# All of gate's block products in matmuls of 512 columns, in one run, with another order of the products

## The chip, the cores and the metric

The kernel runs on one core of a Trainium2 chip. The metric is the device time of one execution in microseconds (us), the median of the runs. The core has a matrix engine (TensorE, PE in the profile; its weight loads are listed apart as PEld), VectorE (DVE), ScalarE (ACT), GpSimd (POOL) and the queues that issue DMA transfers (SP's and POOL's here). Matrix results go to PSUM, of which the kernel uses eight banks of 128 partitions x 512 fp32 columns; everything else stands in SBUF.

## The reference

A decoder trunk of two layers on one sequence of 512 positions and 1024 channels, all in fp32. Each layer has a normalised mixer with a residual and then a normalised gated feed-forward part with a residual. The change touches the feed-forward part alone:

```python
def gated_conv_ffn(x, w_gate, w_up, conv_w, conv_b, w_down):
    g = jnp.einsum('bsd,df->bsf', x, w_gate)
    g = causal_dwconv3(g, conv_w) + conv_b
    up = jnp.einsum('bsd,df->bsf', x, w_up)
    return jnp.einsum('bsf,fd->bsd', jax.nn.silu(g) * up, w_down)
...
        hn = rms_norm(h, norm_ffn[layer])
        h = h + gated_conv_ffn(hn, w_ffn_gate[layer], w_ffn_up[layer], conv_ffn[layer],
                               b_conv_ffn[layer], w_ffn_down[layer])
```

`w_gate` and `w_up` are 1024 x 2816, `w_down` is 2816 x 1024, and `causal_dwconv3` is a convolution over three positions in each channel.

## The kernel before

*Precision.* An fp32 value is held as a high and a low part. A product of two such values is three matmuls that add up in one PSUM bank: high x high, high x low and low x high (`mm3`, lines 154 to 157). A part is made in one of two ways. `halves` (line 721) copies the high part on ACT and subtracts on DVE. `summed` (line 136) writes the negated value on ACT with rounding, adds the value to it by a POOL transfer with addition (line 142), and copies the high part on ACT.

*Tiling.* The 2816 channels are 22 rows of 128. Rows 0 and 1 are computed directly (`direct`). The others are done in pairs, f = 2, 4, ... 20: the 1024 input channels and the 512 positions are cut in two as well, and each of gate (`g`) and up (`u`) becomes a 2x2 block product that takes seven products of blocks instead of eight (Strassen's method in Winograd's form). One product is 256 positions wide and runs over four pairs of channel tiles (`kp` from 0 to 3). After each pair, `half_down` multiplies half of the output channels by four rows done earlier: 48 matmuls of 512 columns, L155 to L157 (two rows and 24 matmuls at f = 2 and 4). Each layer so has ten stages of fourteen block products and a half down projection; the last down products stand behind them (`d_last` in layer 0, a block product at L1262 in layer 1).

*A product* (`multiply`, line 562 on). In the narrow form it is twelve matmuls of 256 columns into the first half of a bank (L577). In the form with `both`, the moving operand holds high and low part side by side, so that one matmul of 512 columns does high x high into the first half of the bank and high x low into the second (L568), and a matmul of 256 columns does low x high (L570); the two alternate over `kp`, four of each. Its second half must be added to the first afterwards. From f = `FIRST_WIDE` = 6 on, products 2, 5 and 3 of both keys take that form.

*Banks.* Each key has three banks for a pair: `BANK` gives "a" to products 1, 6, 7 and 4, "e" to 5 and 3, and "b" to 2. Products of one bank follow each other in it, some of them adding to the sum that stands there; between them the bank is read out. Seven banks circulate (`ps_mm`, line 43) among all matmuls.

*Reading out* (`products`, line 766 on). ACT copies products 1, 6, 7 and 4 of gate into two padded rows and 1, 6 and 7 of up into `kept` (L789). DVE adds product 2 onto 1, the bank of 5 onto 7 and 3 onto 6 (L783), in two additions of 128x256 where the product has two halves. Up's product 4 is read out of its bank by the multiplication with the gate (L813). After products 4 and 3 of gate a row is scaled, convolved (ACT L610, DVE L612) and goes through silu (ACT L620). `split_acts` makes high and low parts of four finished rows at a time (ACT L264, DVE L266).

*Operands.* `block_sums` (line 671 on) makes the moving sums once per layer: `t41` for products 4 and 5, with high and low part side by side, and `t23` for 6 and 7, as one tile of high parts and one of low parts. For `kp` 0 and 1 the low part is made as in `summed` (ACT L692, POOL L693, ACT L694), for 2 and 3 by `halves`. The parts of the plain activations stand in `hg2`, both side by side. `prepare` (line 725) makes the stationary sides of one pair during the stage before it: `a11` (product 1), `s12` (5 and 6), the raw second half (2 and 4, by `summed`) and `s34` (7 and 3), each high and low part of 128x1024, in buffers that circulate by sixes.

*Order.* Every engine and queue runs its instructions in an order fixed when the program is built. A scheduler derives it from the program's order, the data and the buffers; `behind` adds an order between two instructions without a wait on data.

Of the kernel before, what the change touches and what calls it, by code (L numbers as in the profile page):

```python
# [9 lines left out]
F32R = mybir.dt.float32r  # L10
BF16 = mybir.dt.bfloat16
AF = mybir.ActivationFunctionType
ALU = mybir.AluOpType
PSUM = bass.MemoryType.PSUM

P = 128
# [15 lines left out]
def tile_trunk(ctx: ExitStack, tc: tile.TileContext, x, norm_mix, norm_ffn, final_norm,  # L32
# [521 lines left out]
    def multiply(banks, name, product, left, right, both=None):  # L554

        at = BANK[product]  # L560
        first = at not in banks
        if first:
            banks[at] = mm_bank(f"{name}{at}")
        ps = banks[at][:, :HALF]
        if both is not None:
            for kp in range(NP):
                (a_hi, a_lo), last = left(kp), kp == NP - 1
                nc.tensor.matmul(banks[at], a_hi, both(kp), start=first and kp == 0, stop=last,  # L568
                                 skip_group_check=True)
                nc.tensor.matmul(ps, a_lo, right(kp)[0], start=False, stop=last,  # L570
                                 skip_group_check=True)
            return banks[at]
        for kp in range(NP):
            (a_hi, a_lo), (b_hi, b_lo) = left(kp), right(kp)
            for l, r, end in ((a_hi, b_hi, False), (a_hi, b_lo, False),
                              (a_lo, b_hi, kp == NP - 1)):
                nc.tensor.matmul(ps, l, r, start=first, stop=end, skip_group_check=True)  # L577
                first = False
        return ps
# [8 lines left out]
    class Ffn:  # L588
# [81 lines left out]
        def block_sums(self, kp):  # L670
# [14 lines left out]
            self.t23[kp] = self.sums(kp)  # L685
            t41 = self.ap.tile([P, 2, 2, HALF], F32R, name=f"t41_{n}")
            self.t41[kp], self.t41both[kp] = (t41[:, 0], t41[:, 1]), t41
            for (hi, lo), src in ((self.t41[kp], t[:, 2:, :]), (self.t23[kp], t[:, :2, :])):
                if kp > 1:
                    self.halves(hi, lo, src)  # L690
                    continue
                behind(nc.scalar.activation(lo, src, AF.Copy, scale=-1.0), self.first_sums)  # L692
                nc.gpsimd.dma_start(lo, src, accum_op=ALU.add)  # L693
                behind(nc.scalar.activation(hi, src, AF.Copy), self.first_sums)  # L694

        def moving(self, product, kp):
# [3 lines left out]
                c = slice(HALF, S) if product == 3 else slice(0, HALF)  # L700
                return hg[k][0][:, c], hg[k][1][:, c]
            if product in (6, 7):
                return tuple(t[:, product - 6, :] for t in self.t23[kp])
            return tuple(t[:, {4: 0, 5: 1}[product], :] for t in self.t41[kp])

        def moving_both(self, product, kp):
            if product == 5:
                return self.t41both[kp][:, :, 1, :]
            return hg2[kp + NP][:, :, HALF:] if product == 3 else hg2[kp + NP][:, :, :HALF]

        def multiply(self, banks, name, product, weights_, both):
            hi, lo = weights_
# [12 lines left out]
        def prepare(self, f):  # L725
# [12 lines left out]
            for key in "gu":  # L738
# [19 lines left out]
                    c = slice(i * P, (i + 1) * P)  # L758
                    stat[key, product] = hi[:, :, c], lo[:, :, c]
                w = self.unit(f"s34{key}_{n}")  # L760
                self.halves(*w, s34)
                put(key, 7, w, 0)
                put(key, 3, w, 1)
            return stat
# [1 line left out]
        def products(self, f, stat):  # L766
# [6 lines left out]
            dst = {("g", 1): pads[0][:, lo], ("g", 6): pads[0][:, hi], ("g", 7): pads[1][:, hi],  # L773
                   ("g", 4): pads[1][:, lo]}
            dst.update({("u", product): kept[:, i, :] for i, product in enumerate((1, 6, 7))})
            onto = {2: 1, 5: 7, 3: 6}
            s, pending = {}, {}

            wide = f >= FIRST_WIDE

            def add(dst_, ps):
                for half in range(1 + wide):
                    ins = nc.vector.tensor_tensor(dst_, ps[:, half * HALF : (half + 1) * HALF],  # L783
                                                  dst_, ALU.add)
                return ins

            def after(key, product, ps):
                if (key, product) in dst:
                    nc.scalar.copy(dst[key, product], ps)  # L789
                elif product == 5 and (key, 7) not in pending:  # L790
                    pending[key, 5] = ps
                elif product in onto:
                    add(dst[key, onto[product]], ps)
                if (key, product) == ("u", 4):
                    pending["u", 4] = ps
                if product == 7:
                    self.added[key] = add(dst[key, 7], pending[key, 5])

            for key, product in (("g", 1), ("u", 1), ("g", 5), ("g", 6), ("u", 5), ("u", 6),
                                 ("g", 2), ("g", 7), ("u", 2), ("u", 7), ("g", 4), ("g", 3),  # L800
                                 ("u", 4), ("u", 3)):
                after(key, product, self.multiply(banks[key], f"{key}{n}", product,
                                                  stat[key, product],
                                                  wide and product in onto))
                if (key, product) in (("g", 4), ("g", 3)):
                    j = product == 4
                    row = pads[j][:, 2:]
# [2 lines left out]
                    if j and layer == 0:  # L810
                        nc.vector.tensor_tensor(s[1], s[1], self.r, ALU.mult)
            nc.vector.tensor_tensor(s[1][:, HALF:], kept[:, 2, :], s[1][:, HALF:], ALU.mult)
            nc.vector.tensor_tensor(s[1][:, :HALF], pending["u", 4], s[1][:, :HALF], ALU.mult)  # L813
            if layer == 0:
                nc.vector.tensor_tensor(kept[:, :2, :], kept[:, :2, :],
                                        self.r.rearrange("p (a b) -> p a b", a=2), ALU.mult)
# [38 lines left out]
    def ffn0(norm):  # L855
        nonlocal prm1
        with tc.tile_pool(name="f0", bufs=1) as ap:
            def sums(kp):
                return [ap.tile([P, 2, HALF], F32R, name=f"t23{i}_{kp}") for i in "hl"]

            ffn = Ffn(0, prm0, norm, ap, sums)
            def half_down(a, b, half):
# [540 lines left out]
```

## Time and profile before

| | |
|---|---|
| runs | 981.34, 981.38 and 981.81 us, median 981.38 |
| the profiled execution | 981.97 us, its span 980.2 us |
| mean granted TensorE clock | 0.998 |
| instructions | 14798 |
| moved by DMA | 129.27 MB |

The span runs from the first to the last instruction of that one execution, and its own time holds 1.8 us around the span. Busy times of engines overlap, so they don't add up to the span. Matmuls are pipelined, and a matmul's own duration (390 ns for 512 columns) is longer than the time from its start to the next one's; what PE needs for a chain of matmuls is read from start to start.

### The profile page before, as it was taken

To read this page: it belongs to the slowest core of one execution; us is meant where nothing else is said; L and a number is where in the kernel's file an instruction comes from. 1 tells how busy PE (TensorE), PEld (TensorE's weight loads), DVE (VectorE), ACT (ScalarE), POOL (GpSimd) and SP (SyncE) were. 2 spreads that over 40 slices of the span, in tenths; PEclk is the share of its full clock that TensorE was granted. 3 is DMA by queue.
4 is the path that set the end of the run, shared out by engine and by line. 5 is a ranking of instruction groups with operands and counts; after the bars stand their busy time and mean duration, and the time that the engine had idled before them with its cause. 6 is when DMAs were issued, how large, how long until landed. Compare 5 with 4: busy or idle time off the path is not lost.

```text
span 980.2 us, 14798 instructions
## 1 busy us (share of the span) xinstructions
PE 971.0 (99%) x5712; PEld 859.6 (88%) x5712; DVE 808.8 (83%) x1279; ACT 559.2 (57%) x839; POOL 113.0 (12%) x131
## 2 busy tenths in 40 slices
PE   9999999999999999999999999999999999999996
PEld 7888888999988899888889988889989988999885
DVE  5887458998899888997986765599988889878897
ACT  5523347765555564655488734586655455554675
POOL 2141023000000000000210001210000000000022
PEclk9999999999999999999999999999999999999999
DMA  7442225555455455553414623265555554545574
GB/s 249 146 136 86 87 87 129 139 146 147 129 151 135 124 144 136 137 145 107 129 49 117 213 74 103 55 145 132 148 157 137 138 134 124 153 131 147 151 152 128
DMA packets 88371, 129.27 MB, mean 132 GB/s; under 512 B 4485, under 2 KB 58477, under 8 KB 88301
## 3 DMA queue, kind: packets, MB, share of 16 engines
q1 hardware_dynamic: 78316, 98.69, 32.4%
q0 software_dynamic: 8208, 27.79, 15.1%
q10 hardware_dynamic: 1776, 1.84, 0.7%
q8 instruction: 45, 0.74, 0.3%
q14 instruction: 26, 0.20, 0.1%
HBM read 98.42 MB, written 2.10 MB: 103 GB/s over the span
## 4 chain that ended last, share of the span: by engine, by line
PE 92%; DVE 4%; ACT 2%; issue 1%; DMA 0%; POOLq 0%; DVEq 0%; ACTq 0%; POOL 0%
PE d L155 3%; PE dn L155 3%; PE d L156 3%; PE d L157 3%; PE dn L156 3%; PE dn L157 3%; PE gu L155 2%; PE gu L157 1%; PE oo L157 1%; PE oo L155 1%; PE gu L156 1%; PE oe L157 1%; PE oe L155 1%; PE oo L156 1%; PE oe L156 1%; PE u_4a L577 1%
## 5 line engine op out<-in xcount | busy, mean ns | idle before, releaser
L612 DVE SCALAR_TENSOR_TENSOR c<-rows,prm,c 128x512 f32<-128x512 f32 x88 | 65.4, 746 | 2.4 <-ACT c L610 2.3
L142 POOL DMA_DIRECT2D wlo_g<-raw_g x20 | 17.2, 860 | 382.4 <-ACT wlo_g L140 303.0
L155 PE MATMUL d<-a_hi,whi_d 128*128 128x512 f32 x144 | 56.2, 390 | 0.0
L155 PE MATMUL dn<-whi_dn,a_hi 128*128 128x512 f32 x144 | 56.1, 390 | 0.0
L157 PE MATMUL d<-a_hi,wlo_d 128*128 128x512 f32 x144 | 56.1, 389 | 0.0
L156 PE MATMUL d<-a_lo,whi_d 128*128 128x512 f32 x144 | 56.1, 389 | 0.0
L156 PE MATMUL dn<-wlo_dn,a_hi 128*128 128x512 f32 x144 | 56.0, 389 | 0.0
L157 PE MATMUL dn<-whi_dn,a_lo 128*128 128x512 f32 x144 | 56.0, 389 | 0.0
L264 ACT ACTIVATE a_hi<-s 128x512 fp32r<-128x512 f32 x40 | 25.1, 628 | 28.9 <-PE d L157 10.0
L722 ACT ACTIVATE whi_s12u<-s12u 128x1024 fp32r<-128x1024 f32 x20 | 21.2, 1058 | 32.7 <-DVE s12u L744 32.7
L620 ACT ACTIVATE s<-c,prm 128x512 f32<-128x512 f32 x44 | 31.5, 719 | 11.3 <-DVE c L612 11.1
L200 ACT ACTIVATE hg<-h,prm 128x512 fp32r<-128x512 f32 x24 | 17.3, 723 | 36.1 <-DVE h L313 36.1
L723 DVE TENSOR_TENSOR wlo_s34u<-s34u,whi_s34u 128x1024 fp32r<-128x1024 f32 x20 | 24.5, 1225 | 16.1 <-ACT whi_s34u L722 16.1
L151 DVE TENSOR_TENSOR wlo_dn<-raw_dn,whi_dn 128x1024 fp32r<-128x1024 f32 x18 | 22.0, 1225 | 18.7 <-ACT whi_dn L150 18.6
L142 POOL DMA_DIRECT2D wlo_u<-raw_u x21 | 18.1, 860 | 162.2 <-ACT wlo_u L140 132.9
L211 POOL TENSOR_TENSOR ssq_f<-ssq_f,sq_f 128x512 f32<-128x512 f32 x14 | 19.7, 1409 | 133.9 <-ACT sq_f L210 98.9
L201 DVE SCALAR_TENSOR_TENSOR hg<-h,prm,hg 128x512 fp32r<-128x512 f32 x24 | 25.0, 1045 | 11.1 <-ACT hg L200 11.1
L610 ACT ACTIVATE c<-rows,prm 128x512 f32<-128x512 f32 x44 | 31.2, 711 | 2.2 <-DVE rows L808 2.2
L157 PEld LDWEIGHTS d<-a_hi,wlo_d 128*128 128x128 f32 x144 | 27.0, 188 | 5.8
L155 PEld LDWEIGHTS d<-a_hi,whi_d 128*128 128x128 f32 x144 | 27.0, 188 | 5.7
L157 PEld LDWEIGHTS dn<-whi_dn,a_lo 128*128 128x128 f32 x144 | 27.0, 188 | 5.7
L155 PEld LDWEIGHTS dn<-whi_dn,a_hi 128*128 128x128 f32 x144 | 27.0, 188 | 5.7
(1327 smaller groups left out, 3594.0 us busy)
## 6 DMA issues: line engine op xcount, KB each, us to landing
raw_g<-in_w_ffn_gate_dram SPq DMA_DIRECT2D x40, 512.0 KB, 3.8
raw_u<-in_w_ffn_up_dram SPq DMA_DIRECT2D x40, 512.0 KB, 4.1
raw_dn<-in_w_ffn_down_dram SPq DMA_DIRECT2D x22, 512.0 KB, 3.6
wlo_u<-raw_u POOLq DMA_DIRECT2D x21, 512.0 KB, 5.2
wlo_g<-raw_g POOLq DMA_DIRECT2D x20, 512.0 KB, 4.6
raw_d<-in_w_ffn_down_dram SPq DMA_DIRECT2D x18, 512.0 KB, 3.5
raw_oe<-in_w_out_even_dram SPq DMA_DIRECT2D x8, 512.0 KB, 3.5
raw_v<-in_w_in_odd_dram SPq DMA_DIRECT2D x8, 512.0 KB, 4.2
```

Of the source, the lines that this page charges most:

```text
L142: nc.gpsimd.dma_start(lo, raw, accum_op=ALU.add)
L151: behind(nc.vector.tensor_tensor(lo, raw, hi.bitcast(F32), ALU.subtract), after[0])
L155: nc.tensor.matmul(ps, lhs[0], rhs[0], start=start, stop=False)
L156: nc.tensor.matmul(ps, lhs[0], rhs[1], start=False, stop=False)
L157: nc.tensor.matmul(ps, lhs[1], rhs[0], start=False, stop=stop)
L201: nc.vector.scalar_tensor_tensor(hg[k][1], h[k], g, hg[k][0].bitcast(F32), op0=ALU.mult, op1=ALU.subtract)
L264: nc.scalar.activation(hi, src, AF.Copy, scale=scale)
L610: nc.scalar.activation(c, t[:, 0:S], AF.Copy, scale=prm("cf", ft))
L612: nc.vector.scalar_tensor_tensor(c, t[:, i : S + i], prm("cf", i * NF + ft), c, op0=ALU.mult, op1=ALU.add)
L620: nc.scalar.activation(s, c, AF.Silu, bias=self.prm("bf", ft))
L722: nc.scalar.activation(hi, src, AF.Copy)
L723: nc.vector.tensor_tensor(lo, src, hi.bitcast(F32), ALU.subtract)
```

## The change

- `multiply` with `both` issues its four matmuls of 512 columns one after another, and then its four of 256.
- From f = 6 on, all seven products of gate take that form; of up still 2, 5 and 3.
- `t23` becomes one tile for each of products 6 and 7, with high and low part side by side. The splits of those sums are two pieces of 128x256 instead of one of 128x512.
- The fourteen products come in another order.

| | order |
|---|---|
| before | g1 u1 g5 g6 u5 u6 g2 g7 u2 u7 g4 g3 u4 u3 |
| after | g1 u1 g5 g2 g6 u5 u6 u2 g7 u7 g3 u3 g4 u4 |

- Product 5 is copied by ACT and 7 is added onto it by DVE; before it was the other way round. Where a copied product has a second half, DVE adds that half to the copy.
- From f = 6 on, the low part of gate's `s34` is made by a negation on ACT and a POOL transfer with addition, no longer by DVE.
- Up's product 4 is the last one and is still read out of its bank.

```diff
@@ -564,10 +564,10 @@
         ps = banks[at][:, :HALF]
         if both is not None:
             for kp in range(NP):
-                (a_hi, a_lo), last = left(kp), kp == NP - 1
-                nc.tensor.matmul(banks[at], a_hi, both(kp), start=first and kp == 0, stop=last,
-                                 skip_group_check=True)
-                nc.tensor.matmul(ps, a_lo, right(kp)[0], start=False, stop=last,
+                nc.tensor.matmul(banks[at], left(kp)[0], both(kp), start=first and kp == 0,
+                                 stop=kp == NP - 1, skip_group_check=True)
+            for kp in range(NP):
+                nc.tensor.matmul(ps, left(kp)[1], right(kp)[0], start=False, stop=kp == NP - 1,
                                  skip_group_check=True)
             return banks[at]
         for kp in range(NP):
@@ -685,7 +685,8 @@
             self.t23[kp] = self.sums(kp)
             t41 = self.ap.tile([P, 2, 2, HALF], F32R, name=f"t41_{n}")
             self.t41[kp], self.t41both[kp] = (t41[:, 0], t41[:, 1]), t41
-            for (hi, lo), src in ((self.t41[kp], t[:, 2:, :]), (self.t23[kp], t[:, :2, :])):
+            for (hi, lo), src in ((self.t41[kp], t[:, 2:, :]), *(
+                    ((both[:, 0], both[:, 1]), t[:, i, :]) for i, both in enumerate(self.t23[kp]))):
                 if kp > 1:
                     self.halves(hi, lo, src)
                     continue
@@ -700,13 +701,16 @@
                 c = slice(HALF, S) if product == 3 else slice(0, HALF)
                 return hg[k][0][:, c], hg[k][1][:, c]
             if product in (6, 7):
-                return tuple(t[:, product - 6, :] for t in self.t23[kp])
+                t = self.t23[kp][product - 6]
+                return t[:, 0, :], t[:, 1, :]
             return tuple(t[:, {4: 0, 5: 1}[product], :] for t in self.t41[kp])
 
         def moving_both(self, product, kp):
-            if product == 5:
-                return self.t41both[kp][:, :, 1, :]
-            return hg2[kp + NP][:, :, HALF:] if product == 3 else hg2[kp + NP][:, :, :HALF]
+            if product in (6, 7):
+                return self.t23[kp][product - 6]
+            if product in (4, 5):
+                return self.t41both[kp][:, :, product - 4, :]
+            return hg2[kp + NP * (product > 1)][:, :, HALF * (product == 3) :][:, :, :HALF]
 
         def multiply(self, banks, name, product, weights_, both):
             hi, lo = weights_
@@ -758,7 +762,12 @@
                     c = slice(i * P, (i + 1) * P)
                     stat[key, product] = hi[:, :, c], lo[:, :, c]
                 w = self.unit(f"s34{key}_{n}")
-                self.halves(*w, s34)
+                if key == "g" and f >= FIRST_WIDE:
+                    nc.scalar.activation(w[1], s34, AF.Copy, scale=-1.0)
+                    nc.gpsimd.dma_start(w[1], s34, accum_op=ALU.add)
+                    nc.scalar.activation(w[0], s34, AF.Copy)
+                else:
+                    self.halves(*w, s34)
                 put(key, 7, w, 0)
                 put(key, 3, w, 1)
             return stat
@@ -773,35 +782,36 @@
             dst = {("g", 1): pads[0][:, lo], ("g", 6): pads[0][:, hi], ("g", 7): pads[1][:, hi],
                    ("g", 4): pads[1][:, lo]}
             dst.update({("u", product): kept[:, i, :] for i, product in enumerate((1, 6, 7))})
-            onto = {2: 1, 5: 7, 3: 6}
-            s, pending = {}, {}
-
-            wide = f >= FIRST_WIDE
-
-            def add(dst_, ps):
-                for half in range(1 + wide):
-                    ins = nc.vector.tensor_tensor(dst_, ps[:, half * HALF : (half + 1) * HALF],
-                                                  dst_, ALU.add)
+            onto = {2: 1, 7: 7, 3: 6}
+            s = {}
+
+            def in_both(key, product):
+                return f >= FIRST_WIDE and (key == "g" or product in (2, 5, 3))
+
+            def add(d, bank, halves):
+                ins = None
+                for half in halves:
+                    ins = nc.vector.tensor_tensor(d, bank[:, half * HALF : (half + 1) * HALF], d,
+                                                  ALU.add)
                 return ins
 
-            def after(key, product, ps):
-                if (key, product) in dst:
-                    nc.scalar.copy(dst[key, product], ps)
-                elif product == 5 and (key, 7) not in pending:
-                    pending[key, 5] = ps
-                elif product in onto:
-                    add(dst[key, onto[product]], ps)
-                if (key, product) == ("u", 4):
-                    pending["u", 4] = ps
-                if product == 7:
-                    self.added[key] = add(dst[key, 7], pending[key, 5])
-
-            for key, product in (("g", 1), ("u", 1), ("g", 5), ("g", 6), ("u", 5), ("u", 6),
-                                 ("g", 2), ("g", 7), ("u", 2), ("u", 7), ("g", 4), ("g", 3),
-                                 ("u", 4), ("u", 3)):
-                after(key, product, self.multiply(banks[key], f"{key}{n}", product,
-                                                  stat[key, product],
-                                                  wide and product in onto))
+            def after(key, product, bank):
+                halves = range(1 + in_both(key, product))
+                if product in onto:
+                    ins = add(dst[key, onto[product]], bank, halves)
+                    if product == 7:
+                        self.added[key] = ins
+                elif (key, product) != ("u", 4):
+                    d = dst[key, 7 if product == 5 else product]
+                    nc.scalar.copy(d, bank[:, :HALF])
+                    add(d, bank, halves[1:])
+
+            for key, product in (("g", 1), ("u", 1), ("g", 5), ("g", 2), ("g", 6), ("u", 5),
+                                 ("u", 6), ("u", 2), ("g", 7), ("u", 7), ("g", 3), ("u", 3),
+                                 ("g", 4), ("u", 4)):
+                bank = self.multiply(banks[key], f"{key}{n}", product, stat[key, product],
+                                     in_both(key, product))
+                after(key, product, bank)
                 if (key, product) in (("g", 4), ("g", 3)):
                     j = product == 4
                     row = pads[j][:, 2:]
@@ -810,7 +820,7 @@
                     if j and layer == 0:
                         nc.vector.tensor_tensor(s[1], s[1], self.r, ALU.mult)
             nc.vector.tensor_tensor(s[1][:, HALF:], kept[:, 2, :], s[1][:, HALF:], ALU.mult)
-            nc.vector.tensor_tensor(s[1][:, :HALF], pending["u", 4], s[1][:, :HALF], ALU.mult)
+            nc.vector.tensor_tensor(s[1][:, :HALF], bank, s[1][:, :HALF], ALU.mult)
             if layer == 0:
                 nc.vector.tensor_tensor(kept[:, :2, :], kept[:, :2, :],
                                         self.r.rearrange("p (a b) -> p a b", a=2), ALU.mult)
@@ -856,7 +866,7 @@
         nonlocal prm1
         with tc.tile_pool(name="f0", bufs=1) as ap:
             def sums(kp):
-                return [ap.tile([P, 2, HALF], F32R, name=f"t23{i}_{kp}") for i in "hl"]
+                return [ap.tile([P, 2, HALF], F32R, name=f"t{i}_{kp}") for i in (2, 3)]
 
             ffn = Ffn(0, prm0, norm, ap, sums)
             def half_down(a, b, half):
```

## Prediction

> **What bounds the kernel now.** I read the page's busy times first, then its clock row, then the shares of the chain that ended last.
>
> ```profile
> PE 971.0 (99%) x5712; PEld 859.6 (88%) x5712; DVE 808.8 (83%) x1279; ACT 559.2 (57%) x839; POOL 113.0 (12%) x131
> ...
> PEclk9999999999999999999999999999999999999999
> ...
> PE 92%; DVE 4%; ACT 2%; issue 1%; DMA 0%; POOLq 0%; DVEq 0%; ACTq 0%; POOL 0%
> ```
>
> PE is busy in 971.0 of 980.2 us, at full granted clock in every slice, and 92% of the last chain is PE. So time comes off only by shortening PE's slots, and it is lost by any wait that PE gets. Next I cut the table by stage: one gated pair (fourteen block products, then half of a down projection) from its first matmul to the next pair's. The rows are f = 8, 10 and 12 of layer 0; the columns are PE, PEld, DVE, ACT, POOL, then clock, DMA share and GB/s.
>
> ```profile
> 250.38:281.24 30.86, 30.86 (x193) 27.87 (x192) 28.09 (x47) 17.71 (x27) 2.36 (x3) 1.00 0.54 148
> 281.24:312.16 30.92, 30.92 (x193) 27.88 (x192) 28.64 (x47) 16.56 (x24) 1.94 (x3) 1.00 0.61 153
> 312.16:343.05 30.89, 30.89 (x194) 27.90 (x192) 26.71 (x45) 17.74 (x26) 1.50 (x2) 1.00 0.43 120
> ```
>
> A stage is 30.9 us, PE has no gap in it, and DVE has only 2.3 us to spare at f = 10 (30.92 - 28.64). These two facts are the argument: PE's slots give the gain, and DVE's order decides whether PE must wait. The slots themselves are read from the chain of waits at the start of f = 10 (start, length, what).
>
> ```profile
> 281.40 1.43 PE g_10a L577 x12
> 282.84 1.44 PE u_10a L577 x12
> 284.28 0.23 PE g_10e L568
> 284.51 0.12 PE g_10e L570
> 284.63 0.24 PE g_10e L568
> 284.87 0.12 PE g_10e L570
> ...
> 285.57 0.12 PE g_10e L570
> 285.69 1.44 PE g_10a L577 x12
> ```
>
> A narrow product is twelve matmuls of 256 columns: 282.84 to 284.28, 1.44, and 1.43 for the one before, so 1.435 (0.1196 a matmul). A product in both parts, 512 and 256 columns in turn, lasts from 284.28 to 285.69: 1.41.
>
> **The change, part by part.** *The slots.* The window holds eight stages a layer with f from 6, sixteen in all. In each, four products of gate (1, 6, 7, 4) go from twelve matmuls of 256 to four of 512 and four of 256: 64 products. Six more (2, 5, 3 of gate and up) keep their matmuls but get them in a run: 96 products. PE issues 64 x 4 = 256 fewer matmuls and weight loads.
>
> The price of the run form isn't in this trace, and I bound it by neighbours. Matmuls of 512 columns one after another, each with its own weights, stand at the end of layer 1:
>
> ```profile
> 953.02 2.72 PE dn_a L1262 x12
> 955.74 1.36 PE dn_b L1262 x6
> ```
>
> 2.72/12 = 0.2267. A run in which both widths keep their own pace takes 4 x 0.2267 + 4 x 0.1196 = 1.385. If the run gains nothing, it takes the 1.41 of the alternating form. I take 1.392: in the alternating form all four pairs pay the 0.025 between 1.385 and 1.41; in a run only one boundary inside the product is left of the four, a quarter of it. Gain: 64 x (1.435 - 1.392) = 2.75 and 96 x (1.41 - 1.392) = 1.73, together 4.5 us. Bounds: 64 x 0.050 + 96 x 0.025 = 5.6 at 1.385, and 64 x 0.025 = 1.6 at 1.41.
>
> The Trainium skill, page "TensorE: Matmul & The Clock Gate", section "Back-to-back issue gap", gives N/2.4 + 2.5 ns between matmuls in isolation, 215.8 and 109.2 for these widths. By that rule twelve narrow ones take 1.310 and the new form 1.300, in any order: a gain of 0.64 us over 64 products and none over the 96. The trace disagrees: 0.1196 and 0.2267 per matmul are both 10 to 11 ns above the rule, and the alternating form already is 0.025 below the narrow one.
>
> *The banks.* Each wide product leaves a second half to be added. Gate's products 1, 6 and 4 were one ACT copy; now an ACT copy and a DVE addition, in order, free the bank. The bank "a" of gate then takes the next product. Products 5 and 7 swap roles: 5 is copied, 7 added. For both keys DVE gets four more additions of 128x256 in a stage and one subtraction of 128x1024 less:
>
> ```profile
> L783 DVE TENSOR_TENSOR rows<-g_10e,rows x8: 415/420/426, 293.3 to 786.0; 128x256 f32<-128x256 f32 x8
> ...
> L789 ACT COPY rows<-g_10a x8: 353/373/374, 282.9 to 783.9; 128x256 f32<-128x256 f32 x8
> ...
> L723 DVE TENSOR_TENSOR wlo_s34g<-s34g,whi_s34g x20: 1214/1218/1227, 166.0 to 916.9; 128x1024 fp32r<-128x1024 f32 x20
> ...
> L140 ACT ACTIVATE wlo_g<-raw_g x20: 1042/1045/1077, 156.5 to 909.9; 128x1024 fp32r<-128x1024 f32 x20
> ```
>
> 4 x 0.42 - 1.22 = +0.46 us of DVE: 29.1 of some 30.6 us at f = 10. ACT gets the negation, +1.05 on 16.6 to 17.7 of 30.9; its copies stay at seven a stage. Neither sum is a bound by itself. What counts is when gate's product 1 is out of its bank. In the changed program's order its DVE addition stands behind the hidden-state additions, two low parts of the activations and the four sums for up's weights. This trace has that work here (start, length, what, idle before):
>
> ```profile
> 280.46 1.88 DVE L313 TENSOR_TENSOR h<-d,h 128x512 f32<-128x512 f32 x3
> 282.25 1.28 DVE L266 TENSOR_TENSOR a_lo<-s,a_hi 128x512 fp32r<-128x512 f32 x2
> ...
> 285.38 0.69 DVE L756 TENSOR_TENSOR s34u<-raw_u,s12u 128x512 f32<-128x512 f32 x1
> 286.47 1.23 DVE L723 TENSOR_TENSOR wlo_s12u<-s12u,whi_s12u 128x1024 fp32r<-128x1024 f32 x1 [0.40 <-ACT whi_s12u L722]
> ```
>
> The last sum ends at 285.38 + 0.69 = 286.07, the new addition at 286.49. PE needs the bank for gate's product 6 after g1, u1, g5, g2: 281.40 + 1.392 + 1.435 + 2 x 1.392 = 287.01. Slack 0.5 us at f = 10, where activations are split in front; f = 14 and 18 of layer 0 are like it, the other stages have two of those splits less (1.28) and more room. With a low part or two drifting ahead the slack turns into a short wait. I take 0.3 us in each of the three, 1 us in all; bounds: 0, and 1.1 each (3.3), which is what it takes if the 1.23 subtraction goes first (286.47 + 1.23 + 0.42 = 288.1). If PE waits there, up's 5 and 6 are late next, nothing on DVE is. The later gaps are wider: 6 to 7 has three products between (up 5, 6, 2: over 4 us) and 7 to 4 three (up 7, gate 3, up 3).
>
> *The low part by DMA.* Gate's `s34` low part goes from DVE to a negation on ACT and a POOL transfer of 512 KB, between the low parts of gate and up on that queue. It is issued some 1.05 us after ACT's 272.28, and up's at 280.60 keeps its place; the last row here is for up's low parts:
>
> ```profile
> 270.49 0.86 POOL L142 DMA_DIRECT2D wlo_g<-raw_g  x1 [18.82 <-ACT wlo_g L140]
> 280.60 0.86 POOL L142 DMA_DIRECT2D wlo_u<-raw_u  x1 [9.25 <-ACT wlo_u L140]
> ...
> 272.28 1.05 ACT L722 ACTIVATE whi_s34g<-s34g 128x1024 fp32r<-128x1024 f32 x1
> ...
> DMA to landing us min/median/max: 4.5/5.2/8.8
> ```
>
> Issue costs POOL 0.86, it works 2.4 of 30.9 us, and SP's queue isn't touched. Landing by 273.3 + 8.8 = 282.1, gate's 7 starts after eight products, past 292: hidden by 10 us. Up's product 2 is needed one product earlier, after g1, u1, g5, g2, g6, u5, u6: its low part, in the second half of the run, at 281.40 + 2 x 1.435 + 5 x 1.392 + 0.91 = 292.1; at the latest landing it is there at 289.4. Slack 2.7; cost 0, at most 1.9 if it queues a whole 4.6 us behind another transfer (280.60 + 8.8 + 4.6 = 294.0).
>
> *The order.* Up's 4 is last and DVE reads its bank itself; that bank next serves the following pair, behind the half down projection of 10.9 us (48 x 0.2267), so I charge nothing. Gate's 2 comes three products earlier, at 285.6 in this stage; its transfer of 270.49 lands by 279.3. Gate's 4 ends two products later (2.8 us), and with it the odd row's convolution. In layer 0 the same half down projection hides that. At the end of layer 1 the second block operand ends on DVE behind four normalised sums, at 953.72 + 0.42 = 954.14, and is needed by `dn_b` at 955.74: slack 1.6.
>
> ```profile
> 953.72 0.42 DVE L1224 TENSOR_TENSOR hg<-s,hg 128x256 fp32r<-128x256 f32 x1
> ```
>
> The sums ahead of it wait for PE's own last down products, so I charge 0, at most 2.8 - 1.6 = 1.2. The extra splits of the block sums at each layer's start (two more transfers, two more ACT and DVE pieces) come before the first pair; I charge 0, at most 2 x 2 x 0.86 = 3.4 if POOL's issues all show.
>
> *Sum.* -4.5 + 1.0 = -3.5 us. The profiled execution took 981.97 us (span 980.2 and 1.8 around), 0.6 above the median of 981.38. 981.97 - 3.5 = 978.5 for it, and **977.9 us** as a median.
>
> **Rivals.** *A: the run gains nothing.* The slot of a 256 behind a 512 may be what it is because of the load of 128x128 weights, with the same sum in any order. For it: 0.12 follows 0.23 and 0.24 above without a visible loss. Against: 512 columns take 0.2267 behind their like and 0.233 in the alternating form (1.41/4 - 0.1196). Gain 1.6, stalls 1.0: 980.8. Chance 0.15. By the skill's rule above, worked through (0.64 - 1.0): 981.7, chance 0.02.
>
> *B: DVE becomes the bound, slower.* One mechanism: PE's first matmul of gate's product 6 waits for DVE's addition of product 1, behind a queue that is 92% full in layer 0. Price 1.1 us a stage, from the subtraction ahead of it, in all eight stages of layer 0: 8.8 - 4.5 = +4.3, 985.7. In all sixteen: +13.1, 994.5. It decides from 4.5/16 = 0.28 us a stage on. For it: slack 0.5 at f = 10. Against: the other stages have 1.28 more. Chance 0.14.
>
> *C: up's low part comes late.* 1.9 us in the three stages with a late issue, in both layers: 11.4 + 1.0 - 4.5 = +7.9, 989.3. For it: 16 more transfers of 512 KB with SP's loads. Against: 2.7 us of slack, and 7 us between the two issues. Chance 0.05.
>
> *That the change doesn't do what it says*, a run torn apart by the scheduler, isn't so: in the order of the changed program all 160 products stand as four and four.
>
> **How the numbers follow.** My forecast (gain 2 to 6) has 0.64, A and the rule 0.17, B 0.14, C 0.05. The measurement tells no change to about 0.2%, 1.96 us: faster is under 979.4, slower over 983.3. Faster: 0.62 of the forecast, 0.03 of A, 0.01 of B, 0.66. Slower: B 0.12, C 0.05, 0.17. The same: 0.17. The forecast's own range goes from 5.6 with no stall (975.8) to 979.4. With A and small waits of B inside it becomes 975.6 to 982.8; 0.17 lies above, little below.
>
> **What would show it.** After: 16 fewer matmuls in a stage (193 to 177) and a stage of 30.5 to 30.6 us. In the chain, four pieces of 0.23 and then four of 0.12 for every wide product, 1.39 from start to start; 1.41 speaks for A. No idle of PE ahead of gate's 6, but for some tenths at f = 10, 14, 18 of layer 0; a wait there on the addition's line in most stages is B, one ahead of up's 2 or gate's 7 on a POOL transfer is C. DVE's stage sums rise by about 0.5 and POOL issues 20 more transfers. The forecast is wrong if a stage doesn't get shorter by 0.1 or more.

## The result, and the profile after

| | before | after |
|---|---|---|
| median of 8 runs | 981.80 us (981.34 to 982.39) | 978.88 us (978.56 to 979.19) |
| ratio, 95% interval | | 0.9970 (0.9959 to 0.9981) |
| profiled execution, its span | 981.97, 980.2 | 978.92, 977.2 |

The changed kernel is 2.9 us faster; the interval reaches from 1.9 to 4.0 us. The page of the changed kernel, its engines and its chain that ended last:

```profile
PE 966.7 (99%) x5456; PEld 845.6 (87%) x5456; DVE 808.6 (83%) x1331; ACT 575.6 (59%) x867; POOL 130.7 (13%) x151
...
PE 97%; DVE 2%; issue 0%; DMA 0%; ACT 0%; POOLq 0%; DVEq 0%; POOL 0%
```

PE has 256 matmuls less, DVE is as busy as before (808.8), and ACT and POOL are busy 16.4 and 17.7 us longer. The same three stages of layer 0, with the columns PE, PEld, DVE, ACT, POOL, clock, DMA share, GB/s:

```profile
249.94:280.61 30.67, 30.67 (x178) 27.02 (x176) 26.46 (x47) 17.04 (x27) 1.79 (x3) 1.00 0.56 140
280.61:311.27 30.66, 30.66 (x177) 27.03 (x176) 28.93 (x51) 19.27 (x28) 3.37 (x5) 1.00 0.67 170
311.27:341.94 30.67, 30.67 (x177) 27.03 (x176) 26.29 (x47) 16.89 (x26) 1.71 (x3) 1.00 0.56 139
```

A stage went from between 30.86 and 30.92 us down to 30.67, and PE still has no gap in it. The chain of the changed kernel at f = 10 (start, length, what) shows the new slots:

```profile
280.77 0.91 PE g_10a L567 x4
281.68 0.47 PE g_10a L570 x4
282.15 1.44 PE u_10a L577 x12
283.59 0.93 PE g_10e L567 x4
284.52 0.47 PE g_10e L570 x4
284.99 0.93 PE g_10b L567 x4
285.92 0.48 PE g_10b L570 x4
286.40 0.93 PE g_10a L567 x4
...
300.53 0.23 PE d L155
```

A wide product takes 1.40 to 1.41 (283.59 to 284.99, 284.99 to 286.40), and only the first of a stage, behind the down projection's matmuls, takes 1.38. All fourteen take 300.53 - 280.77 = 19.76; before they took 19.97 to 20.00. The sixteen stages together save 3.76 us. That is more than the whole result, so something gave time back. Starts of PE's matmuls in the two timelines say where:

| point on PE | before | after | difference |
|---|---|---|---|
| first pair of layer 0 (f = 2) | 168.25 | 168.05 | -0.20 |
| first wide pair of layer 0 (f = 6) | 219.49 | 219.29 | -0.20 |
| first wide pair of layer 1 (f = 6) | 705.76 | 703.15 | -2.61 |
| first product of the last block product (`dn_a`) | 952.86 | 948.46 | -4.40 |
| second use of that bank | 958.29 | 955.36 | -2.93 |
| end of the span | 980.2 | 977.2 | -3.0 |

Each layer's stages bring 1.8 to 1.9. Half a microsecond more comes between the layers, where PE issues the same matmuls as before; why they take less there was not pursued. And 1.47 us are lost between the first product of `dn_a` and the second use of its bank, 22 us ahead of the end; 1.4 of them (4.40 - 3.0) are still lost at the end of the span. The waits of PE in the changed kernel name the place (what waited, for what, us in total, times, longest):

```profile
PE dn_a L1272 <- DVE y L1172: 0.8, 1, 0.8
```

From PE's last matmul ahead of this wait to its next one 1.24 us pass where 0.23 is usual, so PE stands for 1.0; the other 0.45 of the 1.47 is two matmuls of `dn_e` that it did ahead of their place. In the kernel before PE has no such wait. DVE's timeline in the changed kernel has the cause (start, length, instruction, idle before):

```profile
942.33 1.23 DVE L1209 TENSOR_TENSOR raw_dn<-raw_dn,dnt 128x1024 f32<-128x1024 f32 x1 [1.98 <-issue]
943.47 0.75 DVE L612 SCALAR_TENSOR_TENSOR c<-rows,prm,c 128x512 f32<-128x512 f32 x1
...
954.47 0.75 DVE L1172 SCALAR_TENSOR_TENSOR y<-dn_a,small,y 128x512 f32<-128x512 f32 x1
```

ACT's timeline has the first step of row 21's convolution done at 940.8:

```profile
940.10 0.71 ACT L610 ACTIVATE c<-rows,prm 128x512 f32<-128x512 f32 x1
```

DVE could have gone on with that row then. But its order has a sum of down weights (L1209) ahead of it. That sum overwrites what a POOL transfer reads, and DVE stands for 2 us. The profile names no releaser here (`issue`); that it is the transfer is taken from e3 below, where the profile names it. Everything behind it slides, and the bank of `dn_a` is read at 954.47 although PE had left it at 951.2. In the kernel before, the same sum (L1199 there) stood behind both steps of that row's convolution, and DVE didn't stop:

```profile
945.91 0.75 DVE L612 SCALAR_TENSOR_TENSOR c<-rows,prm,c 128x512 f32<-128x512 f32 x1
...
946.95 1.23 DVE L1199 TENSOR_TENSOR raw_dn<-raw_dn,dnt 128x1024 f32<-128x1024 f32 x1
```

### The profile page after: what moved, and what is told of

It reads as the page before. It is cut to its first block, busy times and chain, and to the rows that moved or that the text cites. A ratio compares the mean times of both kernels' runs of the same rounds, so it can differ in the third digit from the quotient of the medians.

```text
span 977.2 us, 14496 instructions
## 1 busy us (share of the span) xinstructions
PE 966.7 (99%) x5456; PEld 845.6 (87%) x5456; DVE 808.6 (83%) x1331; ACT 575.6 (59%) x867; POOL 130.7 (13%) x151
## 4 chain that ended last, share of the span: by engine, by line
PE 97%; DVE 2%; issue 0%; DMA 0%; ACT 0%; POOLq 0%; DVEq 0%; POOL 0%
PE d L155 3%; PE d L156 3%; PE d L157 3%; PE dn L155 3%; PE dn L156 3%; PE dn L157 3%; PE gu L155 2%; PE gu L157 1%; PE oo L157 1%; PE oo L156 1%; PE gu L156 1%; PE oe L157 1%; PE oe L155 1%; PE oo L155 1%; PE oe L156 1%; PE u_4a L577 1%
## 5 line engine op out<-in xcount | busy, mean ns | idle before, releaser
L726 ACT ACTIVATE whi_a<-raw_g 128x512 fp32r<-128x512 f32 x20 | 12.6, 631 | 57.3 <-PE g_6e L567 7.9
L151 DVE TENSOR_TENSOR wlo_d<-raw_d,whi_d 128x1024 fp32r<-128x1024 f32 x18 | 22.0, 1224 | 13.8 <-ACT whi_d L150 13.8
L726 ACT ACTIVATE whi_s12g<-s12g 128x1024 fp32r<-128x1024 f32 x20 | 21.2, 1061 | 18.0 <-PE g_4e L577 8.7
L201 DVE SCALAR_TENSOR_TENSOR hg<-h,prm,hg 128x512 fp32r<-128x512 f32 x24 | 22.1, 921 | 11.7 <-ACT hg L200 11.7
```

The source lines that it names most:

```text
L151: behind(nc.vector.tensor_tensor(lo, raw, hi.bitcast(F32), ALU.subtract), after[0])
L201: nc.vector.scalar_tensor_tensor(hg[k][1], h[k], g, hg[k][0].bitcast(F32), op0=ALU.mult, op1=ALU.subtract)
```

## The experiments

Ratios are to runs of the kernel before on the same chip (981.9 to 982.04 us there).

| run | median us | ratio (95%) |
|---|---|---|
| e1_run_only | 980.77 | 0.9985 (0.9976 to 0.9994) |
| e2_alternating | 980.88 | 0.9989 (0.9980 to 0.9998) |
| e3_old_order | 981.39 | 0.9996 (0.9987 to 1.0005) |
| e4_low_on_dve | 979.00 | 0.9971 (0.9960 to 0.9981) |
| e5_sum_behind_conv | 977.65 | 0.9956 (0.9943 to 0.9970) |
| e6_wide_from_2 | 1009.61 | 1.0279 (1.0265 to 1.0293) |
| e7_up_wide_too | 979.48 | 0.9979 (0.9970 to 0.9987) |
| e8_both | 1008.39 | 1.0271 (1.0258 to 1.0285) |
| e9_wide_from_2_dve | 1002.61 | 1.0211 (1.0197 to 1.0225) |
| e10_hint_up_wide | 976.17 | 0.9940 (0.9926 to 0.9953) |
| e11_all | 1002.77 | 1.0208 (1.0194 to 1.0222) |

### The run alone, and the wide products alone

e1 is the kernel before with the new loop in `multiply` and nothing else; e2 is the changed kernel with the old loop.

```diff
-                nc.tensor.matmul(banks[at], left(kp)[0], both(kp), start=first and kp == 0,
-                                 stop=kp == NP - 1, skip_group_check=True)
-            for kp in range(NP):
-                nc.tensor.matmul(ps, left(kp)[1], right(kp)[0], start=False, stop=kp == NP - 1,
-                                 skip_group_check=True)
+                (a_hi, a_lo), last = left(kp), kp == NP - 1
+                nc.tensor.matmul(banks[at], a_hi, both(kp), start=first and kp == 0, stop=last,
+                                 skip_group_check=True)
+                nc.tensor.matmul(ps, a_lo, right(kp)[0], start=False, stop=last,
+                                 skip_group_check=True)
```

(The diff is e2's; e1 has it the other way round, against the kernel before.)

> The kernel before with the run form alone: 96 products (2, 5, 3 of both keys, f from 6) change from alternating to a run. Theory (the run saves by itself: 1.413 us in the trace of before, 1.401 in that of after): 96 x 0.012 = -1.2 us against before, 0.07 us a stage. Rival (the run saves nothing and all of the 3.76 us comes from fewer matmuls): 0, a product stays at 1.41.

> The changed kernel with the alternating form in place of the run. Theory: 160 products x 0.012 = 1.9 us slower than the changed kernel, so about 1.0 us faster than before (64 x (1.4375 - 1.413) = 1.6 of gain, less what the end of layer 1 loses). Rival (order inside a product is free): as the changed kernel, 2.9 us faster than before.

Measured: 1.3 and 1.2 us faster than before. In both traces a stage's fourteen products take 19.88, halfway between 19.99 and 19.76: six runs save 0.11 in e1, four products less narrow save 0.11 in e2, and the run of ten saves the other 0.12. From e1's chain:

```profile
283.48 0.93 PE g_10e L567 x4
284.41 0.47 PE g_10e L570 x4
284.88 1.43 PE g_10a L577 x12
```

It is 1.40 where the alternating form had 1.41. In e2 the ten alternating products take (19.88 - 4 x 1.4375)/10 = 1.413 each. Both rivals, that the order inside a product is free and that only the count of matmuls pays, are refuted in the traces, where the two halves add up to the whole 0.23 of a stage. In the medians they are 1.3 and 1.2 of the changed kernel's 2.9. These sizes can't be added so simply: e2 has the wait at `dn_a` too (0.8 us in its trace), e1 doesn't, and each interval is 0.9 us wide to either side.

### The order of the products

e3 is the changed kernel with the list of fourteen as before (and up's product 4 kept by name, as it isn't the last any more).

```diff
-            for key, product in (("g", 1), ("u", 1), ("g", 5), ("g", 2), ("g", 6), ("u", 5),
-                                 ("u", 6), ("u", 2), ("g", 7), ("u", 7), ("g", 3), ("u", 3),
-                                 ("g", 4), ("u", 4)):
+            for key, product in (("g", 1), ("u", 1), ("g", 5), ("g", 6), ("u", 5), ("u", 6),
+                                 ("g", 2), ("g", 7), ("u", 2), ("u", 7), ("g", 4), ("g", 3),
+                                 ("u", 4), ("u", 3)):
```

> The changed kernel with the products in the order of before. Theory (the room between products of a bank covers DVE's late addition): gate's product 6 is due 1.40 us earlier, at 285.0 in the stage f = 10 of layer 0, and its bank is free at about 286.4; PE waits 0.5 to 1.5 us in the stages with splits in front, f = 10, 14, 18 of layer 0, and some tenths in others: 3 to 8 us lost, part of it given back (up to 1.4) because the end of layer 1 gets its last row earlier again; slower than the changed kernel by 2 to 7. Rival (the order does nothing in the stages): no wait of PE on a DVE addition, and 1 to 1.4 us faster than the changed kernel by the end of layer 1.

Measured: 0.65 us faster than before on its chip, so 2.3 of the changed kernel's 2.9 us are lost. That is in the expected range, but not where I expected it. The chain at f = 10:

```profile
283.83 0.93 PE g_10e L567 x4
284.76 0.47 PE g_10e L570 x4
285.23 0.93 PE u_10e L567 x4
286.16 0.12 PE u_10e L570
286.28 0.95 PE g_10a L567 x4
```

The scheduler fills the place: up's product 5 runs while gate's bank is emptied, and the stages of layer 0 take 19.74 to 19.77. The loss is in few places, by its waits:

```profile
PE dn_a L1274 <- DVE y L1174: 1.2, 1, 1.2
PE u_6a L577 <- DVE kept L794: 0.4, 1, 0.4
```

The products of f = 6 in layer 1 take 20.42, 0.7 more than in the changed kernel. And the wait at the end is there too, larger, though gate's product 4 again ends two products sooner. The late row isn't its cause. DVE's timeline at the end of e3 names what is:

```profile
944.68 1.23 DVE L1211 TENSOR_TENSOR raw_dn<-raw_dn,dnt 128x1024 f32<-128x1024 f32 x1 [2.33 <-DMA wlo_dnp<-raw_dn]
945.82 0.75 DVE L612 SCALAR_TENSOR_TENSOR c<-rows,prm,c 128x512 f32<-128x512 f32 x1
```

It is the same sum, ahead of the same convolution, and here the profile names the transfer. The profiled run took 982.35, 1.0 more than e3's median, and its span is 3.4 us longer than the changed kernel's. By the starts on PE, 0.8 of that arises between the layers, 0.8 in layer 1's wide stages (0.7 of it at f = 6), 0.4 up to the second use of the bank of `dn_a` and 1.0 behind it; the rest is small pieces. What costs the time between the layers and behind the bank stays open.

### Gate's low part on DVE again

```diff
-                if key == "g" and f >= FIRST_WIDE:
+                if False:
                     nc.scalar.activation(w[1], s34, AF.Copy, scale=-1.0)
```

> The changed kernel with gate's s34 low part on DVE again (no negation on ACT, 16 transfers less). Theory (DVE is full enough that the 1.22 us it is spared matter): the addition of gate's product 1 comes up to 1.2 us later in stages of layer 0, PE waits 0.3 to 0.7 us in three to eight of them: 1 to 5 us slower than the changed kernel. Rival (DVE's room suffices, the transfer brings nothing): within 0.3 us of the changed kernel, DVE 1.2 us busier in each stage and PE without a gap.

Measured: 979.00, the changed kernel's time. The stage f = 10 of e4:

```profile
280.77:311.44 30.67, 30.67 (x178) 27.02 (x176) 28.71 (x49) 17.68 (x25) 2.18 (x3) 1.00 0.56 148
```

The rival held. At this stage DVE is no busier than in the changed kernel (28.93), because work moved between stages; over the whole run it is 15.7 us busier (824.3 against 808.6), 1.0 in each of the sixteen stages, and PE still has no gap. In this program the low part by DMA is worth nothing that can be measured; it only moves work.

### The end of layer 1

e5 is the changed kernel with the last sum of down weights ordered on DVE behind the last convolution, whose instruction `conv` now remembers.

```diff
-                nc.vector.scalar_tensor_tensor(c, t[:, i : S + i], prm("cf", i * NF + ft), c,
-                                               op0=ALU.mult, op1=ALU.add)
+                self.conved = nc.vector.scalar_tensor_tensor(
+                    c, t[:, i : S + i], prm("cf", i * NF + ft), c, op0=ALU.mult, op1=ALU.add)
...
-            less(b21, b21, t2)
+            behind(nc.vector.tensor_tensor(b21, b21, t2, ALU.subtract), ffn.conved)
```

> The changed kernel with one hint: at the end of layer 1 the last sum of down weights (b21 less t2) is ordered on DVE behind the convolution of row 21. Theory (that sum waits 2 us for a POOL transfer that reads its target, the convolution and all of the last block sums stand behind it in DVE's order, so DVE frees the bank of the first down product late and PE idles 0.97 us): the wait of dn_a on DVE goes, 0.9 to 1.4 us faster than the changed kernel, ratio to before about 0.9958. Rival (the row itself comes too late because gate's product 4 now ends two products later, or DVE has too much to do): the wait stays within 0.3 us of 0.97 and the time is that of the changed kernel.

Measured: 977.65, 1.2 us less than the changed kernel's median (4.25 less than before on its chip, where the changed kernel has 2.92). The intervals of the two ratios overlap, but its slowest run (978.24) is faster than the changed kernel's fastest (978.56), and in its trace PE's wait is gone. DVE's timeline of e5 has the same instructions without the stop, and the bank is read 1.44 us sooner:

```profile
940.99 0.75 DVE L612 SCALAR_TENSOR_TENSOR c<-rows,prm,c 128x512 f32<-128x512 f32 x1 [0.49 <-ACT c L610]
...
942.92 1.22 DVE L1220 TENSOR_TENSOR raw_dn<-raw_dn,dnt 128x1024 f32<-128x1024 f32 x1
...
953.03 0.75 DVE L1172 SCALAR_TENSOR_TENSOR y<-dn_a,small,y 128x512 f32<-128x512 f32 x1
```

### How far DVE carries more wide products

e6 sets `FIRST_WIDE = 2`. e9 does so too but keeps gate's s34 low part on DVE for f below 6. e7 makes all of up's products wide but product 4 (which is read straight from its bank). e8 is e5 and e6 in one, e10 is e5 with e7's rule except in the last pair of layer 1, e11 is e9 and e10.

```diff
-    FIRST_WIDE = 6
+    FIRST_WIDE = 2
```

```diff
-                if key == "g" and f >= FIRST_WIDE:
+                if key == "g" and f >= 6:
```

```diff
-                return f >= FIRST_WIDE and (key == "g" or product in (2, 5, 3))
+                return f >= FIRST_WIDE and (key, product) != ("u", 4)
```

```diff
-                return f >= FIRST_WIDE and (key == "g" or product in (2, 5, 3))
+                return f >= FIRST_WIDE and (key == "g" or product in (2, 5, 3)
+                                            or (product != 4 and (layer, f) != (1, NF - 2)))
```

> The changed kernel with FIRST_WIDE = 2: the stages f = 2 and 4 of both layers take the wide forms too, 28 more products of gate and 12 of up in a run. Theory (a wide product in a run is worth 0.0375 us wherever its operands are there): 40 x 0.0375 = 1.5 us faster than the changed kernel, 20.15 to 19.76 us for the products of these four stages. Rival (at the start of a layer DVE and the transfers are behind, and a wait takes the gain back): products of f = 2 and 4 stay at 20.1 us or more, the same time or slower.

> The changed kernel with the hint at the end of layer 1 and FIRST_WIDE = 2 together. If both are right and independent: 1.0 to 1.4 and 1.5 us, together 2.5 to 2.9 faster than the changed kernel, ratio to before about 0.994. If the two share a wait, less than the sum of the two single ones.

> As e6 (wide forms from f = 2), but gate's s34 low part at f = 2 and 4 stays on DVE. Theory (in e6 the added transfers at f = 2 and 4 wait for their buffers and hold up's low part behind them on POOL's queue): no wait of PE on a POOL transfer, the products of f = 2 and 4 at 19.76 us, 1.5 us faster than the changed kernel. Rival (the additions on DVE at the start of a layer do it): PE still waits on DVE rows at gate's bank a in f = 4 and 6, and it is slower than the changed kernel by several us, as e6 was by 28.

e6 is 27.7 us slower than before, e8 26.5 (1.2 less than e6, which is what the hint brought in e5), e9 20.7. The rivals of e6 and e9 held, and the loss is far larger than I had put it. PE's waits in e9:

```profile
PE u_6b L570 <- DMA wlo_u<-raw_u: 6.4, 2, 3.3
PE g_4a L567 <- DVE rows L794: 5.8, 2, 3.2
PE g_6a L567 <- DVE rows L794: 4.2, 2, 2.6
```

Here is rival B of the prediction, at its very place: PE stands at gate's bank "a" until DVE has added product 1. In e9 no gate transfer was added at f = 2 and 4, and the first wait in time is the one at g_4a (3.2 us, up to 202.59), so the additions start it. DVE itself waited for others for only 0.8 us between 190 and 232. The stages f = 2 and 4 have half the down projection to hide DVE's work. Before the change the two looked like the first pair of rows, and e9's f = 4 like the single row behind them:

```profile
168.25:193.87 25.62, 25.62 (x193) 24.66 (x192) 24.62 (x40) 20.19 (x31) 2.58 (x3) 1.00 0.52 129
193.87:219.49 25.62, 25.62 (x193) 24.66 (x192) 25.22 (x42) 16.26 (x25) 1.72 (x2) 1.00 0.58 151
```

```profile
193.47:222.25 28.78, 25.53 (x154) 22.67 (x153) 27.78 (x50) 16.06 (x25) 1.72 (x2) 1.00 0.51 128
```

DVE was busy 25.22 of 25.62 us at f = 4: ten more additions (sixteen in place of six) of 0.33 to 0.42 don't go in. I could have read that off before the run. The wait for up's low part comes on top, and e6's extra transfers on POOL make 7 us more of it (1009.61 against 1002.61); in e6 PE waits another 6.7 us for up's low part, at f = 4.

> The changed kernel with up's products 1, 6 and 7 in the wide form as well (all but its product 4): 48 more wide products, three more additions of 0.42 us on DVE in each stage. Theory that DVE still has room (no wait of PE in the changed kernel's stages): 48 x 0.0375 = 1.8 us faster than the changed kernel. Rival (DVE becomes the bound: 28.6 + 1.3 of 30.5 us in layer 0): PE waits on DVE additions, 0.5 us or more in each of the eight stages of layer 0, so 2 us slower than the changed kernel or worse, with layer 1 still 0.9 faster.

e7 is no faster than the changed kernel and refutes both sides as stated. All stages up to the last are faster, 19.66 instead of 19.76, those of layer 0 too; what is lost is lost in the last pair of layer 1 and behind it:

```profile
PE g_20a L567 <- DVE rows L794: 0.9, 1, 0.9
PE dn_e L1272 <- DVE y L1172: 0.5, 1, 0.5
PE dn_a L1272 <- DVE y L1172: 0.3, 1, 0.3
```

> e5's hint, and up's products 1, 6 and 7 wide as in e7 but for the last pair of layer 1. Theory (e7 gained 0.10 us a stage and lost it in its last stage alone, 0.9 us at gate's bank a, and at the block product): 15 x 0.10 = 1.5 us faster than e5, ratio to before about 0.994. Rival (DVE's load, not its order at the end, takes the gain): not faster than e5 by more than 0.5 us.

> e9 and e10 together. If both of their theories hold: e10's time less 1.5 to 1.9 us, ratio to before about 0.992; if e9's rival holds, slower than e10.

e10 leaves out the pair that waits and has the hint: 976.17 us, 1.5 less than e5 as expected, 2.7 less than the changed kernel and 5.8 less than before. It beats both kernels, and PE has no wait in its trace from the first pair on. Its stages f = 10 and, with the busiest DVE of layer 0, f = 18:

```profile
280.59:311.16 30.57, 30.57 (x166) 26.39 (x164) 29.12 (x53) 17.87 (x27) 2.41 (x4) 1.00 0.61 152
402.86:433.42 30.56, 30.56 (x165) 26.40 (x164) 29.81 (x54) 18.44 (x27) 3.12 (x4) 1.00 0.64 156
```

e11 adds f = 2 and 4 and loses as much as e9 (1002.77), by waits that are only in part the same: 2.9 us on DVE's rows and 7.3 on up's low part, but 8.4 us on ACT's high part of `s12` for gate's product 5.

## Why the prediction held, point by point

*The bound and the direction.* PE without a gap, paid by the slot: right. 2.9 us came of 3.5 forecast, inside the range, but by terms of which three were off and partly cancel: the slots brought 0.7 less, the waits of 1.0 didn't come, and the end lost 1.5 that I had at 0. Half a microsecond between the layers was in no term. That the sum came so near is partly luck; the mechanism, fewer and cheaper slots on a PE without gaps, is what e1 and e2 show.

*The price of the run.* The term -4.5 was too large; the stages give -3.76. I priced a run at 1.392 from 4 x 0.2267 + 4 x 0.1196 and a quarter of the alternation's 0.025. The runs show 1.40, so a run saves 0.012 of the 0.018 that I gave it: a 512 inside the run takes 0.93/4 = 0.2325, not the 0.2267 of a long row of its like. The share of the fewer matmuls was 64 x (1.4375 - 1.413) = 1.6 (e2's stages: 1.8) and that of the run 160 x 0.012 = 1.9.

The Trainium skill's page "TensorE: Matmul & The Clock Gate", section "Back-to-back issue gap", gives N/2.4 + 2.5 ns for a matmul of N columns in isolation. Worked out from it, as an estimate, the order inside a product is free and 256 matmuls less bring 0.64 us. e1 and e2 disagree: with the same matmuls, the run is worth 0.11 to 0.12 us a stage, and the 256 matmuls less bring 1.8 in e2's stages.

*The waits at gate's product 6.* The term +1.0 was not there: all stages take 19.76 but the first of each layer's wide ones (19.74). The step that failed is what stands ahead on DVE. The changed kernel's timeline at f = 10:

```profile
283.99 0.69 DVE L760 TENSOR_TENSOR s34u<-raw_u,s12u 128x512 f32<-128x512 f32 x1
284.59 0.42 DVE L794 TENSOR_TENSOR rows<-g_10a,rows 128x256 f32<-128x256 f32 x1
```

The addition ends at 285.01 and PE takes the bank at 286.23 in the same timeline: slack 1.2, where I had 0.5. That 0.5 was itself 0.16 too large, because I took PE's start from the chain (281.40) and DVE's times from the timeline, where the stage starts at 281.24; the 2.7 for up's low part has the same flaw. PE reached the bank when I had said, 5.6 us into the stage, but the addition was done after 4.4 us and not after 5.25. The first of the four sums for up's weights had moved ahead of the stage, so that three stand between the splits and the addition. That the bank was where DVE would stop PE is right as a mechanism (e9). How full DVE may be is seen from both sides: 29.81 busy of 30.56 us still goes (e10), ten more additions on top of 25.22 of 25.62 don't (e9).

*DVE's load.* I had it rise by 0.46 us a stage (4 x 0.42 - 1.22). It didn't: 808.6 us in all, after 808.8. e4 shows 1.0 a stage for the subtraction, so the four additions together cost about 1.0 as well, an estimate from these totals, and not 1.68: back to back they start 0.33 to 0.36 us apart, not 0.42.

*The low part by DMA.* Cost 0: right, and e4 shows its gain is 0 too. Up's low parts did get slower to land, but PE waited for none of them:

```profile
wlo_u<-raw_u POOLq DMA_DIRECT2D x21, 512.0 KB, 7.2
```

Before, the median was 5.2; the longest took 9.9, before 8.8. Rival C shows itself in e6 and e9, where PE waits for that transfer; that the late stage pushes it back there is argued and not shown.

*The end of layer 1.* I charged 0, at most 1.2, for the last row's lateness. Measured 1.47 on PE, over that bound. The cause was wrong too: not the row that comes two products later but a sum that the scheduler put ahead of it and that waits for a transfer. e3 has the wait with the early row, e5 hasn't it with the late row. The step that failed is "the sums ahead of it wait for PE's own last down products, so I charge 0": I took DVE's order at the end from the trace of before, where that sum stood behind the convolution, and not from the changed program.

*The start of a layer.* Charged 0: right, the first pairs start 0.2 us from before, and no wait stands there.

## What to carry to other kernels

When PE is full, count its slots from start to start, and then find in each stage which instruction of another engine frees the bank that PE takes next; that one's slack decides, not the engine's busy share. An engine with a fixed order stops for an instruction that was put ahead of its time, and all behind it waits along: here one sum cost 1.2 us of the kernel's time. After a change, read the last stage first, where nothing behind it covers a stop. And before a form is widened to more stages, set the added work against the idle time of the engine that pays for it in those very stages: ten additions of 0.33 us and more into 0.4 us is a no.

## What the runs showed of the hardware

Here, matmuls of 512 columns were slower for a while behind a run of narrower ones. The changed kernel's chain behind up's twelve narrow matmuls:

```profile
269.86 0.23 PE d L155
...
271.48 0.23 PE d L156
...
273.06 0.23 PE d L157
```

The first seven take (271.48 - 269.86)/7 = 0.231, the next seven (273.06 - 271.48)/7 = 0.226. Start by start it is the first five that are slow, 0.232 on average. Before, where an alternating product stood ahead, the same row had 0.227 from its second matmul on. That isn't so everywhere: at f = 10, 14 and 18 of layer 0 the row of before also began slowly, 0.234 over its first seven, though an alternating product stood ahead there too. The width of what stands ahead is thus not the whole of it. The four of a wide product take 0.2325 and so don't leave the slow part, which is where the forecast's 0.7 us went; why they are slower wasn't found out.

A short stop of PE can also cost clock. In e9, windows of 4 us around f = 6 of layer 0 (PE busy is the second number, the clock stands before the DMA share):

```profile
226.00:230.00 4.00, 2.03 (x13) 1.65 (x11) 4.00 (x7) 2.01 (x3) 0.29 (x1) 1.00 0.23 67
230.00:234.00 4.00, 3.39 (x12) 2.91 (x13) 3.47 (x8) 4.00 (x5) 1.43 (x2) 0.69 1.03 313
...
238.00:242.00 4.00, 0.90 (x6) 0.83 (x6) 0.85 (x2) 0.72 (x1) 0.00 (x0) 0.97 0.18 35
242.00:246.00 4.00, 4.00 (x20) 3.66 (x19) 2.23 (x4) 0.00 (x0) 0.00 (x0) 0.60 0.90 285
```

PE stood for 1.97 + 0.61 = 2.6 us over the first two windows and for 3.1 us in the third. The window in which the first stop ended had a mean granted clock of 0.69, the one behind the second stop 0.60. So these waits cost more than themselves. The length of a stop doesn't decide it alone: the 3.2 us at g_4a, which ended at 202.59, were followed by the full clock, and what makes the difference stays open:

```profile
203.00:207.00 4.00, 4.00 (x29) 3.69 (x28) 4.00 (x8) 3.59 (x7) 0.00 (x0) 1.00 1.01 187
```

For e9 the account nearly closes. Its three waits are 16.4 us. The mean granted clock of its profiled run is 0.991 against 0.997 in the changed kernel's, which makes 6 of its 999.7 us, an estimate. Less the 1.5 that forty more wide products save, that is 21 of the 22.5 us by which its span is longer.
